# Key and receptance projections of an RWKV-7 mixer on Trainium2: rounded and low input streamed as one 512-column matmul, the two halves summed afterwards

## Chip, cores and metric

One core of one Trainium2 chip runs the whole program in one launch. The metric is device time in microseconds (us), the median of several executions, lower is better. Before the change it is 1180.07 us (three runs, 1178.05 to 1180.53).

## What is computed

A two-layer model on 256 tokens of width 2048: an RWKV-7 mixer, then sparse attention, in fp32. Only the first mixer is touched, and of it only how its key (k) and receptance (r) projections are summed up and handed on. Cut to what matters:

```python
def rwkv7_mixer(u, v_first, mu, w_rkvz, w0, w1, w2, a0, a1, a2, vres, k_k, k_a, r_k, ln_g, ln_b, w_o):
    xx = token_shift(u) - u
    mixed = u[None] + xx[None] * mu[:, None, None, :]
    rkvz = jnp.einsum('nbtd,nde->nbte', mixed[:4], w_rkvz)
    r, k, v, z = rkvz[0], rkvz[1], rkvz[2], rkvz[3]
    ...
    kk = heads(k * k_k).astype(jnp.float32)
    kk = kk / jnp.maximum(jnp.sqrt(jnp.sum(kk * kk, axis=-1, keepdims=True)), 1e-12)
    k = k * (1.0 + (a - 1.0) * k_a)
    ...
    o = wkv7_scan(rh, heads(decay), kh, vh, -kk, kk * ah.astype(jnp.float32))
```

## The kernel before

**Three products for one.** TensorE works on operands rounded to fp32r. Each fp32 factor is therefore split into a rounded ("high") part, made by ScalarE (L204 for weights: tile `whi`; L418 for inputs), and the remainder ("low"), made by VectorE (L189: `wlo`; L419). A projection sums high times high, high times low and low times high; low times low is dropped. High and low part of one 128-channel slice of the input lie side by side in one tile `mx` of 2 x 256 columns, named `joint[nm, k]` as a whole.

**Two ways to multiply.** `rows_step` (L568, L569, L571; v, z and the later products) loads the input as stationary operand and streams 512 weight columns. `cols_step` loads a 128x128 piece of the weight and streams the 256 tokens, so that the result lies with channels on partitions. Into a 256-column result it issues three matmuls of 256 columns for each of 16 slices (L587 `whi` times high, L588 `whi` times low, L589 `wlo` times high). Into a 512-column result it issues `whi` times the joint tile (512 columns, L593, or L596 for the last slice) and `wlo` times high into the first 256 columns (L594); the two halves are then still to be added. Before the change only the gate projection of the attention layer, late in the program, takes the second way.

**Key stage.** `phase_k(j)` makes block j of 16 (128 channels) in 16 slices. Two blocks share one 512-column bank of PSUM. Between the blocks stand the four blocks `phase_z` of the gate z; the last, `phase_z3`, follows k block 15. Each finished k block feeds `stage_k(j)`, a chain over all engines: ScalarE copies k to SBUF (L683, `ksb`) and squares it (L684, `t`), TensorE sums the squares (L687), VectorE and GpSimd take the power (L695, L696 `rnt`), ScalarE widens it (L702 `rnx`), TensorE turns it (L705), VectorE makes `nk` and `an` (L717 to L719), GpSimd scales (L724, L725 into `sp`), TensorE multiplies (L732), ScalarE copies out (L735 `abs`), and SyncE stores `sp` and `abs` to DRAM (L727 `spd`, L736 `abd`).

**Handover.** Within `phase_z3`, when all 16 chains are issued, the tiles of the scan are opened in the memory of the key stage, and what the scan needs first is loaded: `spl` from `spd` (L883), `invA` from `abd` (L763), `Yb` from `yvd` (L861), all on SyncE's queue, `a` and `t` on GpSimd's (L851, L853). The scan's first matmul (L976) reads `Yb`.

**Scan stage.** Eight pairs U of blocks go through twelve slots each (`phase`, `stats`, `finish`, `prep`, `scale_r`). Between the pieces of a slot `fill(n)` runs n slices of the r projection, block j into bank `rps[j % 2]`, and later of the output projection. `scale_r(U, x)` (slots 1 and 6) takes a finished r block from PSUM and multiplies it twice on VectorE (L964 into `spl`, L965 into `mb`); then GpSimd copies `pc` and makes `ars` (L966, L967).

**What sets the order.** In the key stage the framework orders every engine's instructions by its own timeline estimate. In the scan the order is that of the code, on all engines. In both each engine then runs its list in order, and SyncE's and GpSimd's DMA issues are items of such lists.

Of the kernel before, what the change touches and what calls it, by code (L numbers as in the profile page):

```python
# [10 lines left out]
F32 = mybir.dt.float32  # L11
F32R = mybir.dt.float32r
AF = mybir.ActivationFunctionType
OP = mybir.AluOpType
# [3 lines left out]
T, D, NK = 256, 2048, 16  # L18
# [197 lines left out]
def hybrid_kernel(ctx: ExitStack, tc: tile.TileContext, a: dict, out: bass.AP):  # L216
    nc = tc.nc
    V, S, G, PE = nc.vector, nc.scalar, nc.gpsimd, nc.tensor
# [35 lines left out]
    def accp(name="acc"):  # L254
        n = turn.get(name, 0)
        turn[name] = n + 1
        b = role[name]
        return psum.tile([128, 512], F32, name=f"bank{b[n % len(b)]}", bufs=1)
# [104 lines left out]
    def C(name):  # L363
        o, n = COLS[name]
        return cst[:, o:o + n]
# [17 lines left out]
    KK = prm0[:, 112:128]  # L383
# [197 lines left out]
    def cols_step(o, nm, q, first=True, **kw):  # L581
        wh, wl = W.get()
        for s in range(4):
            k = 4 * q + s
            mh, ml = need((nm, k))
            if o.shape[1] == T:
                PE.matmul(o, wh[:, s, :], mh, start=k == 0 and first, stop=False, **kw)  # L587
                PE.matmul(o, wh[:, s, :], ml, start=False, stop=False, **kw)  # L588
                PE.matmul(o, wl[:, s, :], mh, start=False, stop=k == NK - 1, **kw)  # L589
            else:  # L590
                end = k == NK - 1
                if not end:
                    PE.matmul(o, wh[:, s, :], joint[nm, k], start=k == 0, stop=False, **kw)  # L593
                PE.matmul(o[:, :T], wl[:, s, :], mh, start=False, stop=False, **kw)  # L594
                if end:
                    PE.matmul(o, wh[:, s, :], joint[nm, k], start=False, stop=True, **kw)  # L596
            yield 3 * N256

    def cols_block(nm, o):
        for q in range(4):  # L600
            yield from cols_step(o, nm, q)
# [46 lines left out]
    kph = tc.alloc_tile_pool(name="kph", bufs=1)  # L648
# [5 lines left out]
    kps, w2 = {}, {}  # L654
    kdone, a1done, tdone = set(), set(), set()

    def load_pair(u):
        t = kph.tile([LORA, 2, 256], F32, name="w2s", bufs=2)
        nc.sync.dma_start(t[:, 0, :], a["a_w2"][0][:, u * 256:(u + 1) * 256])
        nc.sync.dma_start(t[:, 1, :], a["a_a2"][0][:, u * 256:(u + 1) * 256])  # L660
        w2[u] = t
# [3 lines left out]
    def stage_k(j):  # L665
        PE, V, S, G = Ranked(nc.tensor, "skPE"), Ranked(nc.vector, "skE"), Ranked(nc.scalar, "skE"), Ranked(nc.gpsimd, "skE")
        yield lambda: j in kdone and (j < KLAG or (j - KLAG) in a1done)
        tmp = lambda name, bufs=2: kph.tile([128, T], F32, name=name, bufs=bufs)
        sp = kph.tile([128, SPW], F32, name="sp", bufs=3)
        BK = sp[:, 0:512].rearrange("p (c x t) -> p c x t", c=NCH, x=2)  # L670
        pp = sp[:, 512:512 + NCH * (CH + 1)].rearrange("p (c t) -> p c t", c=NCH)
        kr = sp[:, SPW - 512:SPW - 256]
        at = sp[:, SPW - 256:]
        w2t = w2[j // 2]
        sc = (j % 2) * 128
        la = accp("la")
        PE.matmul(la[:, :256], w2t[:, 0, sc:sc + 128], hw, start=True, stop=True)
        PE.matmul(la[:, 256:], w2t[:, 1, sc:sc + 128], ha, start=True, stop=True)
        sch.t += 860
        pk = kps.pop(j)  # L680
        ksb = tmp("ksb")
        sqk = tmp("t1")
        S.activation(ksb, pk, AF.Copy)  # L683
        S.activation(sqk, pk, AF.Square, scale=KK[:, j:j + 1])  # L684
        rn = accp("rn")
        for tt in range(2):
            PE.matmul(rn[:, 256 + 2 * tt:258 + 2 * tt], sqk[:, tt * 128:(tt + 1) * 128], C("bo"), start=True, stop=True)  # L687
        sch.t += 430
        yield 400.0
        sst = kph.tile([128, 2, 2], F32, name="sst", bufs=2)  # L690
        rnt = kph.tile([128, 2, 2], F32, name="rnt", bufs=2)
        thw, tha = tmp("thw"), tmp("tha")
        S.activation(thw, la[:, :256], AF.Tanh, scale=0.5, bias=W0H[:, j:j + 1])
        S.activation(tha, la[:, 256:], AF.Tanh, scale=0.5, bias=A0H[:, j:j + 1])
        V.tensor_scalar(sst, rn[:, 256:260].rearrange("p (a b) -> p a b", a=2), 1e-24, None, op0=OP.max)  # L695
        G.tensor_tensor(rnt, sst, half[:, 0:4].rearrange("p (a b) -> p a b", a=2), op=OP.pow)  # L696
        S.activation(thw, thw, AF.Copy, scale=0.5, bias=0.5)
        cum = tmp("cum")
        V.tensor_tensor_scan(cum, C("rst"), thw, 0.0, op0=OP.mult, op1=OP.add)
        yield 1000.0  # L700
        rnx = tmp("rnx")
        S.activation(rnx.rearrange("p (a b n) -> p a b n", a=2, b=2),  # L702
                     rnt[:, :, :, None].to_broadcast([128, 2, 2, 64]), AF.Copy)
        for tt in range(2):
            PE.transpose(rn[:, tt * 128:(tt + 1) * 128], rnx[:, tt * 128:(tt + 1) * 128], ident)  # L705
        sch.t += 215
        G.memset(pp[:, :, 0:1], 1.0)
        S.activation(pp[:, :, 1:], c3(cum), AF.Exp, scale=-DECAY)
        pinv = tmp("pinv")
        S.activation(pinv, cum, AF.Exp, scale=DECAY)  # L710
        an, f = tmp("an"), tmp("f")
        S.activation(an, tha, AF.Copy, scale=-0.5, bias=-0.5)
        S.activation(f, tha, AF.Identity, scale=KAH[:, j:j + 1], bias=KAM[:, j:j + 1])
        V.tensor_tensor(f, ksb, f, op=OP.mult)
        yield 800.0
        nk = tmp("nk")
        V.scalar_tensor_tensor(nk, ksb, KKN[:, j:j + 1], rn[:, :256], op0=OP.mult, op1=OP.mult)  # L717
        V.tensor_tensor(c3(at), c3(nk), pp[:, :, 0:CH], op=OP.mult)
        V.tensor_tensor(an, nk, an, op=OP.mult)  # L719
        S.activation(kr, f, AF.Copy, scale=RK[:, j:j + 1])  # L720
        yield 600.0
        for h in range(2):
            r = slice(64 * h, 64 * h + 64)
            G.tensor_tensor(BK[r, :, h, :], c3(an)[r], c3(pinv)[r], op=OP.mult)  # L724
            G.tensor_tensor(BK[r, :, 1 - h, :], c3(f)[r], c3(pinv)[r], op=OP.mult)  # L725
        yield 2500.0
        nc.sync.dma_start(spd[j], sp)  # L727
        ab = accp("ab")
        for c in range(NCH):
            for h in range(2):  # L730
                r = slice(64 * h, 64 * h + 64)
                PE.matmul(ab[r, c * 64:c * 64 + 64], c3(at)[r, c, :], BK[r, c, h, :], start=True, stop=True)  # L732
        sch.t += 700
        abs_ = tmp("abs")
        S.activation(abs_, ab[:, :256], AF.Copy)  # L735
        nc.sync.dma_start(abd[j], abs_)  # L736
        a1done.add(j)

    kacc = []

    def phase_k(j):
        if j % 2 == 0:
            load_pair(j // 2)
            kacc[:] = [accp("acc")]
        o = kacc[0][:, (j % 2) * 256:(j % 2) * 256 + 256]
        yield from cols_block("k", o)
        kps[j] = o
        kdone.add(j)

    def stage_t(b):  # L750
# [143 lines left out]
    for j in range(16):  # L894
        sch.add(stage_k(j))
# [8 lines left out]
    scan = tc.alloc_tile_pool(name="scan", bufs=1, reuse_waits="tile")  # L904
# [3 lines left out]
    rps = [accp() for _ in range(2)]  # L908
# [8 lines left out]
    mb = one("mb", [128, 2, T])  # L917
# [34 lines left out]
    def parts(U, x):  # L952
        t = SPL[U % 2][x]
        return (t[:, 0:512].rearrange("p (c x t) -> p c x t", c=NCH, x=2),
                t[:, 512:512 + NCH * (CH + 1)].rearrange("p (c t) -> p c t", c=NCH),
                t[:, SPW - 512:SPW - 256],
                t[:, SPW - 256:].rearrange("p (x c t) -> p x c t", x=2, c=NCH))

    def scale_r(U, x):
        if x == 0:  # L960
            PCH[U] = scan.tile([128, 2, NCH], F32, name="pc", bufs=3)
        BK, pp, kr, ar = parts(U, x)
        pr = rps[x][:, 0:256]
        V.tensor_tensor(ar[:, 1], c3(pr), pp[:, :, 1:], op=OP.mult)  # L964
        V.tensor_tensor(mb[:, x], pr, kr, op=OP.mult)  # L965
        G.tensor_copy(PCH[U][:, x], pp[:, :, CH])  # L966
        G.tensor_tensor(ARS[U % 2][x], ar[:, :, 1:, :],  # L967
                        pp[:, None, 0:NCH - 1, CH:CH + 1].to_broadcast([128, 2, NCH - 1, CH]), op=OP.mult)
# [169 lines left out]

    def stream():
        for j in range(NK):  # L1140
            yield from cols_block("r", rps[j % 2][:, 0:256])
        phase_done.add("r")
        banks(acc=(0, 1))
        for nb, k0, k1 in OSEQ:
            yield from o_part(nb, k0, k1)
# [284 lines left out]
    pr = accp("PT")  # L1430
# [284 lines left out]
```

## Time and profile before

| | |
|---|---|
| median of three runs | 1180.07 us (1178.05 to 1180.53) |
| the profiled execution's own time | 1183.66 us |
| its span (first to last instruction) | 1181.6 us |
| mean granted TensorE clock | 0.98 of full |
| busy: TensorE / VectorE / ScalarE / GpSimd | 1133.4 / 861.1 / 711.4 / 344.5 us |
| key stage with z blocks 0 to 2 | 145 to 325 us of the span |
| z block 3 (`phase_z3`) | 325 to 350 us |
| handover, TensorE idle | 350 to 360 us |
| scan with the r projection | 360 to 560 us |

Names in the rows: PE is TensorE, PEld its weight loads, DVE VectorE, ACT ScalarE, POOL GpSimd, SPq SyncE's queue. A row of the timeline has start, duration, engine, line, operation, output<-inputs, shape, and in brackets the idle time before it and what ended it. Matmuls are pipelined: the distance between two starts, not the duration, is what one costs.

### The profile page before, as it was taken

The page shows a single profiled execution, that of the slowest core. Times are in us where ns is not written, and L with a number is a line of the kernel's source. Part 1 is how long each engine was busy: PE and PEld are TensorE (multiplying, and loading weights), DVE is VectorE, ACT ScalarE, POOL GpSimd, SP SyncE. Part 2 cuts the span into 40 slices and gives each one's busy share as a digit, 9 for nine tenths or more (in the row PEclk, how much of TensorE's full clock was granted, in tenths as well). Part 3 has the DMA queues.
Part 4 walks back from the last instruction along what each step waited for, and adds up shares of the span by engine and source line. Part 5 has one row for each costly group of instructions (what it writes and reads, how often), then busy time and mean ns, then how long its engine had stood idle before and what let it go on. Part 6 is the DMA issues. An engine that isn't in the chain of part 4 may idle for free.

```text
span 1181.6 us, 25078 instructions
## 1 busy us (share of the span) xinstructions
PE 1133.4 (96%) x9160; PEld 975.2 (83%) x9160; DVE 861.1 (73%) x1915; ACT 711.4 (60%) x1680; POOL 344.5 (29%) x429
## 2 busy tenths in 40 slices
PE   8999999999986999999989999999999999999997
PEld 7788899887966988888668888787889888988887
DVE  6999877589795786666555868574476888887564
ACT  5667877667763345555445867574556666665553
POOL 1400046234554255654000001100234334344111
PEclk9999999999997999999899999999999999999999
DMA  6558887886888668684346768585655453744753
GB/s 223 172 180 244 239 224 224 227 215 189 261 240 203 182 165 244 181 221 141 99 144 211 248 185 270 167 293 166 183 152 142 126 134 97 191 110 143 287 194 107
DMA packets 232762, 225.22 MB, mean 191 GB/s; under 512 B 51344, under 2 KB 180672, under 8 KB 232256
## 3 DMA queue, kind: packets, MB, share of 16 engines
q1 hardware_dynamic: 228000, 219.01, 63.1%
q0 software_dynamic: 4640, 4.62, 1.7%
q8 instruction: 72, 1.18, 0.4%
q14 instruction: 50, 0.41, 0.1%
HBM read 200.48 MB, written 23.10 MB: 189 GB/s over the span
## 4 chain that ended last, share of the span: by engine, by line
PE 75%; DVE 11%; DMA 4%; issue 3%; ACT 3%; POOL 2%; SPq 1%; ACTq 0%; POOLq 0%; DVEq 0%
PE bank L569 12%; PE bank L568 12%; PE bank L571 12%; PE bank L232 5%; PE bank L593 5%; PE bank L587 4%; PE bank L589 3%; PE bank L588 3%; DVE wlo L189 3%; PE bank L594 3%; PE pair L571 1%; PE pair L568 1%; PE pair L569 1%; DMA invA<-abd 1%; ACT whi L204 1%
## 5 line engine op out<-in xcount | busy, mean ns | idle before, releaser
L189 DVE TENSOR_TENSOR wlo<-wraw,whi 128x512 fp32r<-128x512 f32 (+2 forms) x616 | 442.8, 732 | 145.9 <-ACT whi L204 142.2
L204 ACT ACTIVATE whi<-wraw 128x512 fp32r<-128x512 f32 (+2 forms) x664 | 401.8, 619 | 195.9 <-PE bank L571 96.4
L569 PE MATMUL bank<-wlo,mx 128*128 128x512 f32 (+3 forms) x608 | 230.1, 380 | 5.2 <-DVE wlo L189 5.2
L571 PE MATMUL bank<-whi,mx 128*128 128x512 f32 (+3 forms) x608 | 228.5, 378 | 0.0
L568 PE MATMUL bank<-whi,mx 128*128 128x512 f32 (+3 forms) x608 | 204.1, 379 | 1.2 <-ACT whi L204 1.1
L587 PE MATMUL bank<-mx,whi 128*128 128x256 f32 (+1 forms) x544 | 167.1, 307 | 0.3 <-ACT mx L418 0.3
L589 PE MATMUL bank<-mx,wlo 128*128 128x256 f32 (+1 forms) x544 | 156.2, 288 | 0.6 <-DVE wlo L189 0.6
L588 PE MATMUL bank<-mx,whi 128*128 128x256 f32 (+1 forms) x544 | 156.0, 287 | 0.0
L569 PEld LDWEIGHTS bank<-wlo,mx 128*128 128x128 f32 x608 | 114.8, 189 | 24.4 <-DVE wlo L189 6.7
L568 PEld LDWEIGHTS bank<-whi,mx 128*128 128x128 f32 x608 | 114.1, 189 | 19.9 <-ACT whi L204 1.5
L571 PEld LDWEIGHTS bank<-whi,mx 128*128 128x128 f32 x608 | 114.7, 189 | 17.5
L189 POOL TENSOR_TENSOR wlo<-wraw,whi 128x512 fp32r<-128x512 f32 (+2 forms) x48 | 62.4, 1301 | 168.2 <-ACT whi L204 135.5
L587 PEld LDWEIGHTS bank<-mx,whi 128*128 128x128 f32 (+1 forms) x544 | 104.2, 192 | 5.7 <-ACT mx L418 0.7
L589 PEld LDWEIGHTS bank<-mx,wlo 128*128 128x128 f32 (+1 forms) x544 | 104.4, 192 | 1.9 <-DVE wlo L189 1.0
L588 PEld LDWEIGHTS bank<-mx,whi 128*128 128x128 f32 (+1 forms) x544 | 104.8, 193 | 0.9
L593 PE MATMUL bank<-mx,whi 128*128 128x512 f32 x240 | 87.0, 398 | 0.0
L569 PE MATMUL bank<-wlo,kvh 128*128 128x512 f32 x192 | 76.9, 401 | 0.0
L571 PE MATMUL bank<-whi,kvl 128*128 128x512 f32 x192 | 76.1, 396 | 0.0
L594 PE MATMUL bank<-mx,wlo 128*128 128x256 f32 x256 | 70.7, 285 | 0.0
L568 PE MATMUL bank<-whi,kvh 128*128 128x512 f32 x192 | 67.4, 396 | 0.0
L418 ACT ACTIVATE mx<-mtmp 128x256 fp32r<-128x256 f32 x96 | 39.0, 413 | 28.0 <-DVE mtmp L425 27.3
L593 PEld LDWEIGHTS bank<-mx,whi 128*128 128x128 f32 x240 | 45.1, 188 | 8.8
(332 smaller groups left out, 2087.1 us busy)
## 6 DMA issues: line engine op xcount, KB each, us to landing
wraw<-in_a_w_rkvz_dram SPq DMA_DIRECT2D x128, 512.0 KB, 5.1
wraw<-in_kv_w_dram SPq DMA_DIRECT2D x48, 512.0 KB, 4.5
wraw<-in_b_w_in_dram SPq DMA_DIRECT2D x40, 512.0 KB, 4.1
wraw<-in_a_w_o_dram SPq DMA_DIRECT2D x32, 512.0 KB, 4.5
wraw<-in_b_w_o_dram SPq DMA_DIRECT2D x32, 512.0 KB, 3.6
spd<-sp SPq DMA_DIRECT2D x16, 642.0 KB, 4.7
spl<-spd SPq DMA_DIRECT2D x16, 642.0 KB, 5.9
wraw<-in_b_w_in_dram SPq DMA_DIRECT2D x24, 384.0 KB, 3.3
```

Of the source, the lines that this page charges most:

```text
L189: eng.tensor_tensor(lv, src, hv.bitcast(F32), op=OP.subtract)
L204: self.nc.scalar.activation(hv, src, AF.Copy)
L232: return fn(*args, **kw)
L418: S.activation(h, src, AF.Copy)
L568: PE.matmul(o, mh[:, ts], wh[:, 0, :], start=k == ends[0], stop=False)
L569: PE.matmul(o, mh[:, ts], wl[:, 0, :], start=False, stop=False)
L571: PE.matmul(o, ml[:, ts], wh[:, 0, :], start=False, stop=k == ends[1])
L587: PE.matmul(o, wh[:, s, :], mh, start=k == 0 and first, stop=False, **kw)
L588: PE.matmul(o, wh[:, s, :], ml, start=False, stop=False, **kw)
L589: PE.matmul(o, wl[:, s, :], mh, start=False, stop=k == NK - 1, **kw)
L593: PE.matmul(o, wh[:, s, :], joint[nm, k], start=k == 0, stop=False, **kw)
L594: PE.matmul(o[:, :T], wl[:, s, :], mh, start=False, stop=False, **kw)
```

## The change

k and r blocks now go into whole 512-column banks, so `cols_step` takes its second way for them: per slice one matmul of 512 and one of 256 columns in place of three of 256, and two weight loads in place of three. The halves are added afterwards: for k by a 512-column copy on ScalarE (`k2`) and an add on GpSimd, in `phase_k`, and the chain reads the sum from SBUF; for r by a 256-column copy on ScalarE (`rsum`) and an add on VectorE, in `scale_r`, where the product `mb` moves from VectorE to GpSimd. Line numbers behind the places of the edit shift by up to two.

```diff
@@ stage_k
-        pk = kps.pop(j)
-        ksb = tmp("ksb")
+        ksb = kps.pop(j)
         sqk = tmp("t1")
-        S.activation(ksb, pk, AF.Copy)
-        S.activation(sqk, pk, AF.Square, scale=KK[:, j:j + 1])
+        S.activation(sqk, ksb, AF.Square, scale=KK[:, j:j + 1])
@@ phase_k
         if j % 2 == 0:
             load_pair(j // 2)
-            kacc[:] = [accp("acc")]
-        o = kacc[0][:, (j % 2) * 256:(j % 2) * 256 + 256]
+        o = accp("acc")
         yield from cols_block("k", o)
-        kps[j] = o
+        ksb = kph.tile([128, T], F32, name="ksb", bufs=2)
+        k2 = kph.tile([128, 2 * T], F32, name="k2", bufs=1)
+        S.activation(k2, o, AF.Copy)
+        G.tensor_tensor(ksb, k2[:, :T], k2[:, T:], op=OP.add)
+        kps[j] = ksb
@@ scale_r
-        pr = rps[x][:, 0:256]
+        pr = scan.tile([128, T], F32, name="rsum", bufs=2)
+        S.activation(pr, rps[x][:, T:], AF.Copy)
+        V.tensor_tensor(pr, rps[x][:, :T], pr, op=OP.add)
         V.tensor_tensor(ar[:, 1], c3(pr), pp[:, :, 1:], op=OP.mult)
-        V.tensor_tensor(mb[:, x], pr, kr, op=OP.mult)
+        G.tensor_tensor(mb[:, x], pr, kr, op=OP.mult)
@@ stream
-            yield from cols_block("r", rps[j % 2][:, 0:256])
+            yield from cols_block("r", rps[j % 2])
```

The framework orders the key stage anew. On TensorE, late in `phase_z3`, the matmuls of the last chain (j = 15, L732, output `bank_4337`) stood here before, among z's matmuls (outputs `bank_4211` and `bank_4212`):

```order
L568 MATMUL bank_4211<-whi,mx_1329 128x512
L568 MATMUL bank_4212<-whi,mx_1329 128x512
L732 MATMUL bank_4337<-sp 64x64
L569 MATMUL bank_4211<-wlo,mx_1329 128x512
L571 MATMUL bank_4211<-whi,mx_1329 128x512
L569 MATMUL bank_4212<-wlo,mx_1329 128x512
L732 MATMUL bank_4337<-sp 64x64 x7
```

and in the changed kernel (there L730, `bank_4121`; z's outputs are `bank_3997` and `bank_3998`; L977 is the scan's first matmul):

```order
L730 MATMUL bank_4121<-sp 64x64 x7
L569 MATMUL bank_3997<-wlo,mx_1361 128x512
L571 MATMUL bank_3997<-whi,mx_1361 128x512
L569 MATMUL bank_3998<-wlo,mx_1361 128x512
L571 MATMUL bank_3998<-whi,mx_1361 128x512
L568 MATMUL bank_3997<-whi,mx_1376 128x512
L569 MATMUL bank_3997<-wlo,mx_1376 128x512
L571 MATMUL bank_3997<-whi,mx_1376 128x512
L568 MATMUL bank_3998<-whi,mx_1376 128x512
L569 MATMUL bank_3998<-wlo,mx_1376 128x512
L571 MATMUL bank_3998<-whi,mx_1376 128x512
L977 MATMUL pair_4429<-Yb_4225,a_4221 64x32 x16
```

Of the 96 matmuls of `phase_z3`, 77 stood ahead of the end of the last chain's matmuls (two of them even ahead of k block 15's end) and 19 behind it; now 86 stand ahead and 10 behind.

On GpSimd, the end of the key stage before (L696 is a chain's power, L725 and L724 its two scalings, L880 the first memset of the handover):

```order
L724 TENSOR_TENSOR sp<-an,pinv 64x4x64 x4
L725 TENSOR_TENSOR sp<-f,pinv 64x4x64 x2
L696 TENSOR_TENSOR rnt<-sst,half 128x4
L724 TENSOR_TENSOR sp<-an,pinv 64x4x64 x2
L880 MEMSET a_4437 128x512
```

and now (L694 is the power, L723 and L722 the scalings, L745 the new add; this one is that of block 15):

```order
L745 TENSOR_TENSOR ksb<-k_3994 128x256
L722 TENSOR_TENSOR sp<-an,pinv 64x4x64 x2
L723 TENSOR_TENSOR sp<-f,pinv 64x4x64 x2
L722 TENSOR_TENSOR sp<-an,pinv 64x4x64 x2
L694 TENSOR_TENSOR rnt<-sst,half 128x4
L722 TENSOR_TENSOR sp<-an,pinv 64x4x64 x2
L879 MEMSET a_4221 128x512
```

The add of a block stands in the same list as the scalings of the chains ahead of it (here of blocks 13, 14 and 15), and the chain of its own block starts behind it.

On SyncE's queue, around the store of the last chain's `abs`, before:

```order
L736 DMA abd<-abs 128x256 x2
L176 DMA wraw<-in_a_w_rkvz_dram 128x8x128 x3
L727 DMA spd<-sp 128x1284
L176 DMA wraw<-in_a_w_rkvz_dram 128x8x128 x2
L736 DMA abd<-abs 128x256
L883 DMA spl_4442<-spd 128x1284
L883 DMA spl_4443<-spd 128x1284
```

and now (L725 stores `sp`, L734 `abs`, L882 loads `spl`):

```order
L734 DMA abd<-abs 128x256
L176 DMA wraw<-in_a_w_rkvz_dram 128x8x128
L725 DMA spd<-sp 128x1284
L176 DMA wraw<-in_a_w_rkvz_dram 128x8x128 x2
L734 DMA abd<-abs 128x256
L882 DMA spl_4226<-spd 128x1284
L882 DMA spl_4227<-spd 128x1284
```

The neighbours of the last store are the same kinds; six loads of r weights (`wraw`) now stand ahead of it in all, where five did. In the scan the order is the old one but for the edited instructions, and ahead of the key stage and behind the scan nothing has moved.

More of the change, by code (lines that the diff above doesn't have):

```diff
@@ L737, in stage_k @@
         a1done.add(j)
-    kacc = []
     def phase_k(j):
```

## Prediction

> **What bounds the kernel now.** I read the page's busy times first, then the table of stretches around the two stages that change, then the handover between them row by row.
>
> ```profile
> span 1181.6 us, 25078 instructions
> PE 1133.4 (96%) x9160; PEld 975.2 (83%) x9160; DVE 861.1 (73%) x1915; ACT 711.4 (60%) x1680; POOL 344.5 (29%) x429
> ```
>
> TensorE is busy for 96% of the span. Where it is not idle, its work sets the time; whatever shortens that work counts only up to the next wait that something else ends.
>
> ```profile
> 145.00:325.00 180.00, 175.13 (x1318) 158.23 (x1317) 138.83 (x261) 125.71 (x286) 77.38 (x89) 1.00 0.78 223
> 325.00:350.00 25.00, 25.00 (x148) 19.65 (x146) 24.22 (x49) 17.23 (x40) 13.05 (x18) 1.00 0.81 236
> 350.00:361.00 11.00, 0.69 (x4) 0.28 (x2) 2.85 (x7) 2.20 (x5) 7.84 (x15) 0.66 0.88 232
> 361.00:385.00 24.00, 20.09 (x227) 19.12 (x228) 16.66 (x58) 8.92 (x18) 8.69 (x17) 0.86 0.85 200
> 385.00:560.00 175.00, 169.70 (x3269) 151.13 (x3267) 119.12 (x314) 90.59 (x264) 86.56 (x143) 0.97 0.70 190
> ```
>
> Columns: stretch, length, busy time of PE, PEld, DVE, ACT, POOL, granted TensorE clock, DMA share, GB/s. Key stage, z block 3, handover, the scan's start, the scan. The key stage and the scan are bound by TensorE (4.9 of 180 and 5.3 of 175 us idle). The third row is different: TensorE does next to nothing for 10 us. What ends that:
>
> ```profile
> 324.66 0.28 PE L589 MATMUL bank<-mx,wlo 128*128 128x256 f32 x1
> ...
> 345.92 0.37 ACT L735 ACTIVATE abs<-bank 128x256 f32<-128x256 f32 x1
> 346.65 0.53 SPq L736 DMA_DIRECT2D abd<-abs  x1
> 349.91 0.39 PE L571 MATMUL bank<-whi,mx 128*128 128x512 f32 x1
> 352.97 0.32 SPq L883 DMA_DIRECT2D spl<-spd  x1
> 353.82 5.96 DMA invA<-abd
> 360.28 0.39 PE L976 MATMUL pair<-Yb,a 64*64 64x32 f32 x2 [9.98 <-DMA Yb<-yvd]
> ```
>
> k block 15 ends at 324.66. Its chain ends with `abs` at 345.92; the store of it goes out at 346.65; the second load of `spl` (its memory lies over `abs`) goes out only at 352.97, when that store has landed; then `invA` and `Yb` behind it, and the scan starts at 360.28. z block 3 was done at 349.91, so the scan's start hangs on the last chain: 13.6 us behind its store, whatever TensorE has saved before.
>
> **The price of one slice.** Three 256-column matmuls as they stand in the key stage, and the new form as the attention layer already uses it:
>
> ```profile
> 203.01 0.28 PE L589 MATMUL bank<-mx,wlo 128*128 128x256 f32 x1
> 203.13 0.28 PE L587 MATMUL bank<-mx,whi 128*128 128x256 f32 x1
> 203.25 0.28 PE L588 MATMUL bank<-mx,whi 128*128 128x256 f32 x1
> 203.37 0.28 PE L589 MATMUL bank<-mx,wlo 128*128 128x256 f32 x1
> ...
> 989.91 0.39 PE L593 MATMUL bank<-mx,whi 128*128 128x512 f32 x1
> 990.14 0.28 PE L594 MATMUL bank<-mx,wlo 128*128 128x256 f32 x1
> 990.26 0.39 PE L593 MATMUL bank<-mx,whi 128*128 128x512 f32 x1
> ```
>
> Start to start: 0.36 us for three; 0.23 + 0.12 = 0.35 us for the pair. The columns are the same 768, so only about 10 ns per slice are to be had: 512 columns at 0.23 cost 10 ns less than twice 0.12. The weight load that drops out lay beside the matmuls and is worth nothing by itself. A saving of a third, as the count of instructions suggests, is not on offer. The number of slices, from the key stage (145 to 340 us) and from the scan (361 to 561 us):
>
> ```profile
> L587 PE MATMUL bank<-mx,whi 128*128 128x256 f32 x256 | 75.1, 293 | 0.0
> ...
> L587 PE MATMUL bank<-mx,whi 128*128 128x256 f32 x256 | 82.8, 323 | 0.0
> ```
>
> So at most 256 x 10 ns = 2.6 us in each stage.
>
> [...]
>
> **Key stage: what is added.**
>
> ```profile
> L683 ACT ACTIVATE ksb<-bank x16: 362/366/385, 151.4 to 325.9; 128x256 f32<-128x256 f32 x16
> L684 ACT ACTIVATE t<-bank,prm x16: 461/468/477, 151.6 to 326.2; 128x256 f32<-128x256 f32 x16
> L888 ACT ACTIVATE vt<-bank x1: 599/599/599, 349.7 to 349.7; 128x512 f32<-128x512 f32 x1
> L1471 POOL TENSOR_TENSOR zT<-zT,RST x16: 727/746/1196, 863.4 to 1084.0; 128x256 f32<-128x256 f32 x16
> L724 POOL TENSOR_TENSOR sp<-an,pinv x32: 728/1062/2922, 162.1 to 342.1; 64x256 f32<-64x256 f32 x32
> L719 DVE TENSOR_TENSOR an<-nk,an x16: 410/418/966, 160.5 to 339.8; 128x256 f32<-128x256 f32 x16
> ```
>
> (Durations are lowest/median/highest in ns.) Per block ScalarE swaps a 0.37 us copy for a 512-column one of 0.60: 16 x 0.23 = 3.7 us more, beside TensorE, on an engine with 54 us free of 180. GpSimd gets 16 adds of 0.75 us, 12 us, on an engine with 100 free. What lies on the chain: 0.60 + 0.75 in place of 0.37, so each chain gets about 1.0 us longer before the square (0.47, as before). The edges of the add are 0.73 and, queued behind a pair of scalings, 2 x 2.9 more. By the new order the squares' matmul stands some 28 to 31 matmuls of the next block behind its own block's end, about 14 slices or 5 us; 0.60 + 0.75 + 0.47 fits in with 3 us to spare, so TensorE should not wait there. Blocks in whole banks: no wait of TensorE in this stretch names a bank's release, so I take zero both ways. The waits it does have:
>
> ```profile
> PE bank L732 <- POOL sp L724: 1.7, 2, 1.3
> PE bank L687 <- ACT t L684: 1.3, 2, 1.1
> PE bank L705 <- ACT rnx L702: 1.2, 2, 0.8
> ```
>
> (Who waited for whom, total us, times, longest.) 4.2 us; the new order could remove all of them or, with a busier GpSimd, double them. I take no change, and keep -4.2 and +4.2 for the range.
>
> The handover then decides what of the 2.6 us arrives. Ahead of the last chain's last matmul TensorE does 256 cheaper slices (-2.6 us) but nine more matmuls of z block 3 (86 in place of 77, 9 x 0.23 = +2.1 us). So the store of `abs` goes out about 0.5 us sooner, and the scan starts 0.5 us sooner; z block 3 ends 2.6 us sooner, and the idle time grows from 10 to about 12 us. The sixth weight load ahead of that store waits for VectorE's low part of the first r piece, made beside z block 3 while the matmuls run; I take zero and, if it is late, up to the 3 us that VectorE (24.2 of 25 us busy there) could be behind. The memsets and loads of GpSimd at the handover hold `t`, which the scan needs only after its first step. **Key stage: -0.5 us.**
>
> **Scan: what is added.**
>
> ```profile
> 382.52 0.41 DVE L964 TENSOR_TENSOR spl<-bank,spl 128x256 f32<-128x256 f32 x1
> 383.32 0.27 PE L1011 MATMUL bank<-spl 64*64 64x64 f32 x2 [1.87 <-DVE mb L965]
> ...
> 420.70 0.70 ACT L1111 ACTIVATE O<-pair,nmr,rg 128x64 f32<-128x64 f32 x2 [1.83 <-DVE nmr L1097]
> 425.25 0.49 PE L1049 MATMUL pair<-X,Yb 64*64 64x64 f32 x8 [0.75 <-DVE sta L1079]
> ...
> 384.00:388.00 4.00, 4.00 (x63) 3.71 (x58) 3.73 (x14) 0.97 (x2) 1.02 (x3) 0.57 0.37 99
> 424.00:430.00 6.00, 5.25 (x82) 4.62 (x80) 4.00 (x11) 3.46 (x12) 0.00 (x0) 0.72 0.48 151
> ```
>
> VectorE does two passes of 0.41 us per block as before: the add comes in, `mb` goes out. ScalarE's copy (0.37 us, as L683) stands in slot 1 ahead of the `O` pieces, where ScalarE sat idle for 1.83 us until `nmr` was there, and in slot 6 behind `X`; 16 x 0.37 = 6 us on an engine with 84 free of 175. If that cover is gone, 8 x 0.37 = 3 us at the most. The bank is now free after copy and add, not after both products: at 383.32 TensorE waited for `mb`; it should wait about 0.4 us less. GpSimd's `mb` costs 16 x 0.75 = 12 us of its 88 free, and is read six slots later. Its one price: VectorE's 128x256 product took 0.42 us as a rule and 0.97 at worst, beside GpSimd; 16 such blows are 8.8 us of VectorE's time, of which only what falls into the few slots where TensorE waits for VectorE counts, as at 425.25. I take 0.4 us, with 0 and 2 as ends.
>
> Of the 2.6 us of the slices I take off what falls under half clock behind such waits (the last two rows, 0.57 and 0.72 granted) and into those slots, about a fifth: -2.1 us. With the 0.4: **scan -1.7 us.**
>
> Sum: -0.5 - 1.7 = -2.2 us, on a span of 1181.6 or an own time of 1183.66 us. That execution was 3.6 us over the median of the runs; taken from the median the forecast is 1180.07 - 2.2 = 1177.9 us. Measurement can tell about 0.2%, 2.4 us: below 1177.7 counts as faster, above 1182.4 as slower.
>
> **Rivals.**
>
> *The key stage's saving arrives too.* If half of the 4.2 us of waits go (the squares' matmul stands later than before), the last chain ends 2 us sooner still: 1175.8. For it: the new places are later. Against: the other two waits, on L705 and L732, are no nearer to gone.
>
> *GpSimd makes the last chain late (slower).* GpSimd runs its list in order. The add of a block stands among scalings that take up to 2.9 us each and that wait for VectorE's `an`:
>
> ```profile
> POOL sp L724 <- DVE an L719: 24.2, 10, 7.9
> ```
>
> An add behind such a wait holds the block's own chain; five or more blocks late by a microsecond push the store of `abs` back by 5 us, and the scan with it: 1177.9 + 0.5 + 5 = 1183.4. It decides from a store about 4 us later than in the forecast, near 350 us. Against: the order leaves 3 us of room at each block.
>
> [...]
>
> [...]
>
> **How the numbers follow.** The forecast 0.48, its own range 1176.3 to 1179.5 (the key stage's waits by 1, the scan's terms by 0.6); the saving arriving too 0.20; GpSimd late 0.22; nothing saved 0.10. Faster: 0.20 of the first, 0.19 of the second: 0.39. Slower: 0.20 of the third and 0.02 of the last: 0.22. The rest, 0.39, is within 0.2%. The range leaves a tenth on each side: 1175.0 to 1183.4.
>
> **What would show it.** In the profile after: pairs 0.35 us apart; z block 3 done near 347 us, the store of `abs` near 346 and the scan's first matmul near 359.8, with 12 us of idle ahead of it; waits of L685 on `t` gone; the r projection done some 2 us sooner relative to the scan's start. The prediction is wrong if TensorE waits for GpSimd's `ksb` in the key stage, if the store of `abs` leaves after 349, or if VectorE's waits in slot 3 grow past a microsecond more in sum.

## The result, and the profile after

The changed kernel took 1194.78 us (median of four runs, 1193.8 to 1200.13), the kernel before 1180.3 us beside it: ratio 1.0127, 95% interval 1.0102 to 1.0152. The forecast was 1177.9, its range ended at 1183.4. The change costs 14.5 us. Two single runs of the experiments below, 1213.6 us with `mb` back on VectorE and 5806 us in the last combined kernel, lie far off the others of their kernels and are left out of the figures.

The profiled execution took 1200.13 us, 5 to 6 us more than the other three; 2 us of that lie ahead of the key stage, where the two kernels do the same. Its span and busy times:

```profile
span 1198.4 us, 24104 instructions
PE 1134.9 (95%) x8648; PEld 944.4 (79%) x8648; DVE 865.6 (72%) x1915; ACT 717.1 (60%) x1696; POOL 379.2 (32%) x461
```

512 matmuls fewer, and TensorE is as busy as before. A second execution of it (1194.06 us, span 1192.3) is nearer to the median; its table of stretches, in the columns of the table of before (length, busy time of PE, PEld, DVE, ACT, POOL, granted clock, DMA share, GB/s):

```profile
145.00:321.20 176.20, 172.49 (x1050) 143.60 (x1049) 137.71 (x255) 123.83 (x276) 89.38 (x100) 0.99 0.78 222
321.20:349.80 28.60, 27.80 (x159) 21.51 (x158) 26.33 (x55) 19.34 (x47) 16.54 (x20) 1.00 0.75 226
349.80:362.60 12.80, 0.20 (x1) 0.00 (x0) 3.42 (x8) 2.84 (x6) 10.24 (x19) 0.60 0.94 256
362.60:386.40 23.80, 18.82 (x150) 15.32 (x150) 15.38 (x53) 9.19 (x20) 7.12 (x13) 0.86 0.79 161
386.40:570.00 183.60, 173.58 (x3090) 138.04 (x3090) 124.81 (x318) 94.44 (x276) 103.11 (x160) 0.95 0.70 183
```

Row by row against before: the key stage is 3.5 us shorter (179.7 to 176.2); z block 3 is 3.3 us longer (25.25 to 28.6), the idle time from its end to the scan's first matmul 2.7 us longer (10.37 to 13.03), and so the scan starts 2.4 us later, where it was to start 0.5 us sooner. Then the last row: TensorE idles 10.0 us in it instead of 5.3, and its granted clock is 0.95 instead of 0.97. So most of the loss is in the scan; from the end of the r projection to the end of the program the two take the same (622.2 and 622.5 us).

The key stage and the handover in the first profile, start and duration:

```profile
170.05 0.39 PE L593 MATMUL bank<-mx,whi 128*128 128x512 f32 x1
170.28 0.28 PE L594 MATMUL bank<-mx,wlo 128*128 128x256 f32 x1
170.40 0.39 PE L593 MATMUL bank<-mx,whi 128*128 128x512 f32 x1
...
324.75 0.40 PE L596 MATMUL bank<-mx,whi 128*128 128x512 f32 x1
...
352.43 0.37 ACT L733 ACTIVATE abs<-bank 128x256 f32<-128x256 f32 x1
353.17 1.34 SPq L734 DMA_DIRECT2D abd<-abs  x1
353.18 0.39 PE L571 MATMUL bank<-whi,mx 128*128 128x512 f32 x1
...
366.46 0.39 PE L977 MATMUL pair<-Yb,a 64*64 64x32 f32 x2 [12.89 <-DMA Yb<-yvd]
```

The pair costs 0.35 us, as forecast. The last `abs` comes 27.7 us behind the last slice of k (21.3 before), and the scan's first matmul 13.3 us behind the store (13.6 before).

Now one round of the scan where it goes wrong, in the first profile. GpSimd first, `mb` of slot 6 to `rg`; then VectorE, ScalarE and TensorE behind it (bracket: idle time and what ended it):

```profile
412.25 0.92 POOL L966 TENSOR_TENSOR mb<-rsum,spl 128x256 f32<-128x256 f32 x1 [8.50 <-issue]
...
414.70 0.59 POOL L850 DMA_DIRECT2D a<-abd  x1
...
418.51 0.55 POOL L852 DMA_DIRECT2D t<-tnd  x1
419.39 1.09 POOL L860 DMA_DIRECT2D Yb<-yvd  x2 [0.33 <-PE pair L1050]
421.93 0.55 POOL L860 DMA_DIRECT2D Yb<-yvd  x1 [1.45 <-DMA a<-abd]
423.76 2.82 POOL L860 DMA_DIRECT2D Yb<-yvd  x5 [1.28 <-DMA vt<-vd]
426.59 2.08 POOL L1091 TENSOR_TENSOR rg<-rg,half 128x8 f32<-128x8 f32 x1
```

```profile
424.13 0.17 DVE L1090 TENSOR_SCALAR rg<-mv 128x8 f32<-128x8 f32 x1
...
428.70 0.17 DVE L1098 SCALAR_TENSOR_TENSOR nmr<-mv,rg 128x8 f32<-128x8 f32 x1 [1.57 <-POOL rg L1091]
...
430.06 0.28 DVE L1064 COPY S<-pair 128x128 f32<-128x128 f32 x1
```

```profile
428.90 0.70 ACT L1112 ACTIVATE O<-pair,nmr,rg 128x64 f32<-128x64 f32 x2 [3.31 <-DVE nmr L1098]
...
430.39 0.56 PE L1043 MATMUL pair<-S,ars 64*64 64x64 f32 x16 [2.25 <-DVE S L1064]
```

In the kernel before, the same eight `Yb` loads went out in one piece and `rg` found GpSimd waiting for it:

```profile
413.02 4.33 POOL L861 DMA_DIRECT2D Yb<-yvd  x8 [2.17 <-PE pair L1049]
418.02 2.05 POOL L1090 TENSOR_TENSOR rg<-rg,half 128x8 f32<-128x8 f32 x1 [0.67 <-DVE rg L1089]
```

So `mb` stands ahead of eight DMA issues, these stand ahead of eight more, and `rg` stands behind them all. And in the trace the second eight wait for landings: the four loads of `a` took 2.8 to 7.0 us from issue to landing, and GpSimd stood idle 1.45 us ahead of the third load of `Yb` until one of them had landed, and 1.28 us ahead of the fourth, which the profile puts down to a landing of `vt`. From 385 to 560 us its waits ahead of loads of `Yb` that ended with a landing of `a` sum up to 4.2 us in the first profile and 6.0 in the second, and to 0.9 in the kernel before. Why the issue of one load waits for the landing of another was not shown.

This seemed to be the whole cause. The first four runs showed that it was not.

### The profile page after: what moved, and what is told of

Same layout as the page of the kernel before. It is cut to its first block, busy times and chain, and to the rows that moved or that the text cites. A ratio compares the mean times of both kernels' runs of the same rounds, so it can differ in the third digit from the quotient of the medians.

```text
span 1198.4 us, 24104 instructions
## 1 busy us (share of the span) xinstructions
PE 1134.9 (95%) x8648; PEld 944.4 (79%) x8648; DVE 865.6 (72%) x1915; ACT 717.1 (60%) x1696; POOL 379.2 (32%) x461
## 4 chain that ended last, share of the span: by engine, by line
PE 53%; DMA 4%; DVE 2%; issue 2%; ACT 2%; POOL 1%; SPq 0%; POOLq 0%; ACTq 0%; DVEq 0%
PE bank L569 9%; PE bank L571 9%; PE bank L568 9%; PE bank L593 7%; PE bank L232 5%; PE bank L594 3%; DMA a<-abd 2%; DMA Yb<-yvd 1%; PE pair L571 1%; PE pair L568 1%; PE pair L569 1%; DVE wlo L189 1%; POOL Yb L860 1%; ACT whi L204 1%; PE pair L1056 1%
## 5 line engine op out<-in xcount | busy, mean ns | idle before, releaser
L593 PE MATMUL bank<-mx,whi 128*128 128x512 f32 x720 | 276.9, 418 | 0.0
L594 PE MATMUL bank<-mx,wlo 128*128 128x256 f32 x768 | 214.0, 288 | 3.8 <-DVE wlo L189 3.8
L568 PE MATMUL bank<-whi,mx 128*128 128x512 f32 (+3 forms) x608 | 204.7, 379 | 1.4 <-ACT mx L418 0.9
L593 PEld LDWEIGHTS bank<-mx,whi 128*128 128x128 f32 x720 | 137.8, 192 | 29.3
L594 PEld LDWEIGHTS bank<-mx,wlo 128*128 128x128 f32 x768 | 147.9, 193 | 9.4 <-DVE wlo L189 5.0
L425 DVE SCALAR_TENSOR_TENSOR mtmp<-xx,prm,xn 128x256 f32<-128x256 f32 x96 | 48.6, 519 | 1.1 <-POOL xx L457 1.0
L569 PEld LDWEIGHTS bank<-wlo,kvh 128*128 128x128 f32 x192 | 36.1, 188 | 8.5 <-issue 0.4
L419 DVE TENSOR_TENSOR mx<-mtmp,mx 128x256 fp32r<-128x256 f32 x96 | 41.5, 442 | 1.4 <-ACT mx L418 1.4
L1045 ACT ACTIVATE X<-pair 128x128 f32<-128x128 f32 x32 | 8.9, 279 | 56.0 <-PE pair L1043 33.9
L571 PEld LDWEIGHTS bank<-whi,kvl 128*128 128x128 f32 x192 | 36.2, 188 | 7.4
```

The lines of the kernel that those rows point to most:

```text
L419: V.tensor_tensor(l, src, h.bitcast(F32), op=OP.subtract)
L425: V.scalar_tensor_tensor(m, xx[:, k, :], mu[:, k:k + 1], xn[:, k, 1:], op0=OP.mult, op1=OP.add)
L568: PE.matmul(o, mh[:, ts], wh[:, 0, :], start=k == ends[0], stop=False)
L569: PE.matmul(o, mh[:, ts], wl[:, 0, :], start=False, stop=False)
L571: PE.matmul(o, ml[:, ts], wh[:, 0, :], start=False, stop=k == ends[1])
```

## The experiments

Each was timed beside the kernel before (its medians there 1180.2 to 1181.4); the ratio is to that. "r stretch" is first to last matmul of the r projection: 195.0 us in the first profile of before, 206.0 and 203.0 in the two of the changed kernel.

### The parts alone

**Key part alone**: the edits in `scale_r` and `stream` undone.

> The key projection as changed, the receptance projection as before. Theory 1: the scan keeps its old pace (r projection 195 us from the scan's first matmul), and only the later scan start of about 4 us is left: 1184 us. If the later last abs does not matter, as a rival has it (the scan's start was late in that one execution alone): 1180 us.

1182.1 us, ratio 1.0006 (0.9987 to 1.0025): no change that the runs can tell, and between the two expectations. In its profile k takes 175.8 us, the last `abs` comes at 348.5, the scan starts at 362.55, the r stretch is 192.5. So the key stage does save 3.8 us, and the handover takes more than that back: counted from the start of k, the last `abs` comes 2.2 us later than before and the scan starts 1.8 us later.

**Receptance part alone**: the edits in `stage_k` and `phase_k` undone.

> The receptance projection as changed, the key projection as before. Theory 1: the scan starts where it did (360 us), the r projection takes 206 us: 1190.5 us (1189 to 1192). If the scan's slower pace comes from its later start or from what the key stage left behind, it is gone here: 1180 us or less.

1188.5 us, 1.0056 (1.0035 to 1.0077). The scan starts at 360.3 and the r stretch is 199.6: slower, if by less than expected. The cost is 7 us, the key part's 0.7, and the two together cost 14.5: they do not add up. The scan from 23.8 us behind its start, in the columns of the table above and with as many matmuls as its last row (this execution took 1185.8 us):

```profile
384.10:564.60 180.50, 168.58 (x3090) 134.31 (x3090) 125.10 (x319) 94.23 (x276) 103.05 (x160) 0.98 0.71 186
```

TensorE idles 11.9 us of it.

### The scan: two causes, each hiding the other

**`mb` back on VectorE.**

```diff
-        G.tensor_tensor(mb[:, x], pr, kr, op=OP.mult)
+        V.tensor_tensor(mb[:, x], pr, kr, op=OP.mult)
```

> The changed kernel with one line undone: the product mb is back on VectorE; the r halves are still summed behind TensorE, the key stage is as changed. Theory 1 (GpSimd's list): mb's 0.9 us on GpSimd holds the scan's loads of a and Yb and then the power of rg behind them; without it the r projection takes about 195 us from the scan's first matmul instead of 206, and the time is near 1184 us (1182 to 1186). Theory 2 (the longer link): the ScalarE copy and the VectorE add of the halves hold the scan; then this edit, which puts a third pass on VectorE, gains nothing: 1193 us or more. [...]

1193.6 us, 1.0105 (1.006 to 1.015). Theory 1 alone falls, the time is the one that theory 2 expected: the r stretch is 200.8, TensorE's waits for `Yb` within the scan are down to 1.1 us (5.2 and 3.1 in the two profiles of the changed kernel), but it waits 4.8 us for `S` and 7.4 us for `sta`.

**GpSimd's part of slot 6 behind the loads** (in part; `scale_g` holds the three GpSimd operations, the comment is added here).

```diff
             if v == 6 and U + 2 < NU:
                 load_a(U + 2)
+            if v == 6 and U + 1 < NU:
+                scale_g(U + 1, 1)    # mb, pc, ars of the second half
```

> The changed kernel, with the same work on every engine, but in slot 6 GpSimd's three operations of the second half (mb, pc, ars) stand behind the eight DMA issues of a and t instead of ahead of them. Theory 1: the loads go out as early as before, Yb and rg follow in time, and the scan's loss of about 11 us goes but for 1 to 3: 1186 us (1184 to 1188). [...]

1197.8 us, 1.0134 (1.0094 to 1.0175), r stretch 204.7. No gain either. What still holds the scan is seen in slot 1; the kernel before first, then the kernel with `mb` on VectorE:

```profile
523.24 0.42 DVE L964 TENSOR_TENSOR spl<-bank,spl 128x256 f32<-128x256 f32 x1
...
524.16 0.57 ACT L1051 ACTIVATE uv<-pair 64x128 f32<-64x128 f32 x2 [0.73 <-PE pair L1049]
526.14 0.17 DVE L1097 SCALAR_TENSOR_TENSOR nmr<-mv,rg 128x8 f32<-128x8 f32 x1 [1.55 <-POOL rg L1090]
...
526.82 0.28 DVE L1063 COPY S<-pair 128x128 f32<-128x128 f32 x1
```

```profile
505.72 0.57 ACT L1052 ACTIVATE uv<-pair 64x128 f32<-64x128 f32 x2 [0.72 <-PE pair L1050]
506.32 0.39 ACT L963 ACTIVATE rsum<-bank 128x256 f32<-128x256 f32 x1
506.73 0.42 DVE L964 TENSOR_TENSOR rsum<-bank,rsum 128x256 f32<-128x256 f32 x1 [1.81 <-ACT rsum L963]
...
508.47 0.16 DVE L1098 SCALAR_TENSOR_TENSOR nmr<-mv,rg 128x8 f32<-128x8 f32 x1
...
509.15 0.28 DVE L1064 COPY S<-pair 128x128 f32<-128x128 f32 x1
```

Before, VectorE's products started 0.9 us ahead of `uv`. Now ScalarE's copy of the second half stands behind `uv`, which waits for TensorE; VectorE idles 1.81 us for it, and `S` follows `uv` by 3.43 us instead of 2.66 (in this kernel VectorE's third pass stands in between as well). The last matmul of the r block had started at 502.63, 3.7 us ahead of the copy: nothing but the place in ScalarE's list makes the copy wait.

**The copy for slot 1 one slot earlier; and that with `mb` on VectorE** (in part; `scale_r` then takes this copy and makes none of its own in slot 1, the comment is added here).

```diff
                 if U + 1 < NU:
+                    copy_r(U + 1, 0)     # S.activation(rsum, rps[0][:, T:], AF.Copy)
                     load_v(U + 1)
```

> The changed kernel, with the ScalarE copy of the r half for slot 1 made one slot earlier, behind X and ahead of uv, since the r block is complete by then; mb stays on GpSimd. Theory 4 (the copy's place in ScalarE's list): in the changed kernel the copy stands behind uv, which waits for TensorE, so VectorE idles some 1.8 us ahead of its add in each round and nmr, S and O come late; with the early copy these waits of VectorE for rsum go (8.4 us in sum), and what is left is GpSimd's mb ahead of the loads and of rg: the r projection takes 198 to 202 us instead of 206, the time is 1187 to 1191 us. Theory 1 (GpSimd alone): no change, 1194 us or more.

1195.7 us, 1.0109 (1.0077 to 1.0141), r stretch 203.4. VectorE's waits for `rsum` in the rounds are gone, but now `nmr` waits for `rg` (7.8 us in sum from 385 to 560 us, 0.5 in the second profile of the changed kernel). The gain is smaller than theory 4 expected; `mb` still stands ahead of the loads.

The second kernel has this and the edit of `mb` above.

> The changed kernel with both: the copy for slot 1 made one slot earlier, and mb back on VectorE. Theory 4 with 1 (two causes, each of which keeps the scan late when the other is taken away): the r projection takes 192 to 195 us, and only the key stage's part is left: 1180 to 1182 us. If a third pass of VectorE per block is what counts (theory 5): 1188 us or more, with VectorE busy without idle time between rg and S.

1185.05 us, 1.0052 (1.0026 to 1.0079), r stretch 192.8. No cure by itself gained more than some 5 us of the stretch, and none gained time that the runs can tell; the two together gain 10 us of the stretch at the least and 10 us of time.

**Both moved, the work on every engine unchanged**: the early copy, and GpSimd's part of slot 6 behind the loads.

> The changed kernel with two moves and the same work on every engine: the ScalarE copy for slot 1 one slot earlier, and GpSimd's mb, pc and ars of slot 6 behind the DMA issues of a and t. mb stays on GpSimd. If GpSimd's part of the loss is only that mb stands ahead of these loads: the r projection takes 193 to 197 us, the time is 1185 to 1188 us, as with mb back on VectorE (192.8, 1185). [...]

1180.8 us, 0.9985 (0.9967 to 1.0003), r stretch 191.0. `mb` is on GpSimd, all operations are those of the change, and 14 us are gone by two moves, one of a copy and one of GpSimd's three operations. So `mb`'s own time on GpSimd does not count wherever it stands; its place was the mistake. The time is 4 us better than with `mb` on VectorE, but there `pc` and `ars` stayed ahead of the loads, and how much of the 4 us is theirs was not tested. The stretches of this kernel from the scan's start, the second one with the same 3090 matmuls as the last row of the changed kernel's table:

```profile
361.50:385.25 23.75, 19.19 (x164) 15.64 (x168) 15.64 (x54) 9.28 (x20) 7.09 (x13) 0.85 0.68 161
385.25:556.60 171.35, 166.51 (x3090) 132.89 (x3082) 128.65 (x318) 93.87 (x276) 100.07 (x160) 0.99 0.72 196
```

Against 183.6 us in the changed kernel: TensorE idles 4.8 us instead of 10.0, and the granted clock is 0.99 instead of 0.95, so that the same matmuls take 166.5 us of busy time instead of 173.6 (166.5 x 0.99 / 0.95 = 173.5). Of the 12.3 us, 5.2 are idle time and 7.1 are clock. And who waits for whom from 385 to 560 us, in the changed kernel (second profile) and in this one (total us, times, longest):

```profile
ACT O L1112 <- DVE nmr L1098: 8.8, 5, 2.2
DVE rsum L964 <- ACT rsum L963: 8.4, 5, 1.8
POOL Yb L860 <- DMA a<-abd: 6.0, 4, 2.5
PE pair L1050 <- DVE sta L1080: 5.2, 4, 2.2
```

```profile
POOL Yb L860 <- PE pair L1065: 23.3, 6, 5.0
ACT O L1127 <- DVE nmr L1113: 4.5, 6, 1.9
PE pair L1065 <- DVE sta L1095: 2.7, 4, 1.4
```

The loads of `Yb` now wait for TensorE to release their tile, and no longer for a landing. So it was in the kernel before:

```profile
POOL Yb L861 <- PE pair L1049: 11.2, 6, 2.2
```

**Receptance alone, with `mb` on VectorE and the early copy** (k as before, and the two edits shown).

> The key projection as before; the receptance projection as changed, with the early copy and mb on VectorE. If the two halves of the change add up: the scan starts at 360 us as in the kernel before, the r projection takes 192.5 us, and the time is 1178 us (1177 to 1179.5). If the scan's saving comes only together with the changed key stage, or the copy of the second half costs as much as it brings: 1180 us or more.

1185.0 us, 1.0027 (1.0014 to 1.004), r stretch 197.9: with `mb` on VectorE the receptance part does not pay even without the key part. Whether VectorE's third pass does it, or `pc` and `ars` ahead of the loads, no run separates.

**Receptance alone, with both moves** (k as before).

> The key projection as before; the receptance projection as changed, with the early ScalarE copy and GpSimd's mb, pc, ars of slot 6 behind the loads. The scan starts where it did, at 360 us; the r projection takes 191 to 193.5 us; the slices' 2 us arrive: 1178.5 us (1177 to 1180) against 1180.5 for the kernel before. If the saving of the scan comes only with the changed key stage ahead of it: 1181 us or more.

1178.4 us, 0.9978 (0.9965 to 0.9991), r stretch 190.3: the receptance part by itself, with its operations in these places, pays about 2.6 us.

### The key stage and its handover

In the three kernels of this section the receptance projection is as before.

**Halves added on VectorE.**

```diff
-        S.activation(k2, o, AF.Copy)
-        G.tensor_tensor(ksb, k2[:, :T], k2[:, T:], op=OP.add)
+        S.activation(ksb, o[:, T:], AF.Copy)
+        V.tensor_tensor(ksb, o[:, :T], ksb, op=OP.add)
```

> Only the key projection is changed, and its halves are added on VectorE (ScalarE copies 256 columns, VectorE adds them to the bank) instead of a 512-column copy on ScalarE and an add on GpSimd. In the order that the framework makes of it, 26 matmuls of z block 3 stand behind the last chain's, where 10 did with the GpSimd add and 19 in the kernel before. Theory A (the gain of the key stage is eaten at the handover by the last chain's place): the key stage keeps its 3.8 us, the last abs comes some 5 us earlier than in the kernel before, and the scan starts 3 to 5 us earlier: 1176 to 1178 us. Theory B (VectorE, not GpSimd, is short in z block 3): no gain, 1181 us or more.

1180.1 us, 1.000 (0.9984 to 1.0017). The last `abs` comes sooner than with GpSimd's add (346.5 against 348.5), though not sooner than before (345.9): the key stage is 2.7 us longer than with GpSimd's add (178.5), and TensorE waits in it once 3.9 us for `wlo` (2.6 with GpSimd's add). And the scan starts at 362.8 all the same, 15.8 us behind the store instead of 13.3. Neither theory: one part of the gain is paid for ahead of the handover, the other within it.

**Last block as before.**

```diff
-        yield from cols_block("k", o)
+        last = j == NK - 1
+        yield from cols_block("k", o[:, :T] if last else o)
...
+        if last:
+            S.activation(ksb, o[:, :T], AF.Copy)
```

> Only the key projection is changed, but its last block (j = 15) is summed on TensorE as before, with three matmuls a slice, and has neither the 512-column copy nor the GpSimd add on its chain. Its order puts only 5 matmuls of z block 3 behind the last chain's (10 with all blocks changed, 19 before). If the last chain's own copy and add make the handover late: the last abs comes 1 us or more earlier than with all blocks changed, 1180 us or less. If the order of TensorE's list does it: the last abs comes about 1 us later still, 1183 us.

1187.3 us, 1.0056 (1.0036 to 1.0075). The last `abs` comes 2.7 us later than with all blocks changed, counted from the start of k, though its chain has neither the 512-column copy nor the add: it is not these that make the handover late. The five further matmuls of z ahead of the last chain's end account for 1.2 us, and `abs` itself comes 1.1 us later behind its matmuls on ScalarE. The time is 4 us worse than that order explains; its profile, of an execution of 1184.7 us, does not show where.

**Last four blocks on VectorE.**

```diff
+        if j >= 12:
+            S.activation(ksb, o[:, T:], AF.Copy)
+            V.tensor_tensor(ksb, o[:, :T], ksb, op=OP.add)
+        else:
```

> Only the key projection is changed; the halves of blocks 0 to 11 are added on GpSimd as in the change, those of blocks 12 to 15 on VectorE (256-column copy and an add from the bank). In the order that results, 24 matmuls of z block 3 stand behind the last chain's, 10 with all adds on GpSimd, 19 before. Theory A (the place of the last chain in TensorE's list sets the scan's start): the key stage keeps its 3.5 us, the last abs comes about 3 us sooner than with all adds on GpSimd, the scan starts near 359.5 us instead of 362.6: 1178 to 1180 us. Theory B (the chain is late by GpSimd's and ScalarE's own work, not by that place): the scan starts at 362 us or later, 1182 us.

The last `abs` comes at 342.7, 4.3 us sooner counted from the start of k than with all adds on GpSimd, as theory A says, but the store and the loads behind it take longer:

```profile
343.35 1.03 SPq L734 DMA_DIRECT2D abd<-abs  x1
345.95 0.37 SPq L176 DMA_DIRECT2D wraw<-in_a_w_rkvz_dram  x1
346.41 4.21 SPq L886 DMA_DIRECT2D spl<-spd  x2
...
359.00 0.72 PE L979 MATMUL pair<-Yb,a 64*64 64x32 f32 x4 [11.74 <-DMA Yb<-yvd]
```

From store to scan it is 15.7 us instead of 13.3; the scan starts 2.1 us sooner. The time does not show even that: 1182.8 us, 1.0005 (0.9988 to 1.0022), where the profiled execution took 1178.5. So the key part is worth nothing in three of its four forms and costs some 7 us in the fourth, and what keeps the scan's earlier start out of the time stays open. A sooner store is at least not handed on in full: here and with all halves added on VectorE the scan starts 15.7 and 15.8 us behind it. The record does not show why.

### Together, and the baselines

Both parts; every key add on VectorE, the early copy, `mb` on VectorE:

> Both projections changed; the key halves added on VectorE, the receptance with the early copy and mb on VectorE. Key part alone measured 1180.1 against 1180.2 before; if the receptance part brings its 2 us on top: 1178 us. If the two parts disturb each other as in the changed kernel: 1183 us or more.

1186.1 us, 1.0031 (1.001 to 1.0053), r stretch 196.7: with `mb` on VectorE again no gain.

Both parts; the last four key adds on VectorE, the early copy, GpSimd's part of slot 6 behind the loads:

> Both projections as changed, with all mends: key adds of the last four blocks on VectorE; in the scan the early ScalarE copy, and GpSimd's three operations of slot 6 behind the loads. With all mends but the first it took 1180.8 us. If the mends add up: 1177 us (1176 to 1179). If the last chain's place brings nothing: 1180.5 us.

1179.6 us, 0.9982 (0.9969 to 0.9995): 2 us faster than before, but no better than the receptance part alone.

The changed kernel, and the kernel before, once more:

> The changed kernel once more, for a second profile of it (the first one fell on the longest of its four runs). Both theories: about 1194.5 us; the r projection takes 202 to 206 us from its first matmul, VectorE waits some 8 us for the rsum copy, and the scan starts 13 to 14 us behind the last abs.

1194.9 us, r stretch 203.0, VectorE's waits for `rsum` 8.4 us, the scan 13.8 us behind the last `abs`: as expected. It is the profile quoted as the second one above.

> The kernel before once more, for a second profile of it, since the first one took 3.6 us more than the median. Expected 1180 us; the scan's first matmul at 360 us as in the first profile; the r projection 190.5 to 193 us from its first matmul, less than the 195 of the first profile, if the forecast's own size for the scan's saving (1.7 us) is right; 195 us if the saving is 4.

One run, 1182.5 us; the scan's first matmul at 362.2, 215.5 us behind the start of k (215.3 in the first profile), r stretch 191.3. The first profile's 195.0 was long; the unchanged scan code gave 190.6 to 195.2 in six profiles (before twice, and the four kernels with the key part alone). A difference of under 5 us in one stretch of one profile is therefore no evidence here, and the conclusions above rest on the times.

## Why the prediction was wrong

- **The slice, and its sum: right, a little small.** Pairs 0.35 us apart; over the key stage the median distances in the traces are three times 120 ns before and 234 and 117 ns now, 9 ns less per slice, and in the scan a slice takes 7 ns less in the mean (415 in the kernel before, 408 with both moves, at full clock). The 0.10 on "nothing saved" supposed a slice that gains next to nothing; no run shows that, the traces show the 9 and 7 ns. The key stage is 3.5 us shorter in the second profile and 3.8 with the key part alone, but 2.0 in the first profile, instead of 2.6; of the 3.5, 1.2 are waits of TensorE that went (4.9 us idle before, 3.7 now; the rival "the saving arrives too" had this half right).
- **The handover: wrong in sign.** The step was "nine more matmuls of z block 3 (...) = +2.1 us". From the last slice of k to the last `abs` it is 6.6 us more in the second profile (27.8 against 21.3): 11 more matmuls of z from that point with their spacing, 3.2 us; eight more matmuls of other kinds and the spacing of the chains' own, 1.4; waits, 0.8, for VectorE's `wlo`; `abs` itself 1.2 later behind its matmuls on ScalarE. I counted one kind of matmul and took the rest of the list, and the waits in it, as equal. The store left at 349.6 and 353.2 in the two profiles, past the 349 that I had named as a sign, and the scan started 2.4 us later. Nor do the 13.6 us from store to scan hold "whatever TensorE has saved before": they were 15.7 and 15.8 in two kernels above.
- **`mb` on GpSimd: the step that failed.** "GpSimd's `mb` costs 16 x 0.75 = 12 us of its 88 free, and is read six slots later. Its one price: VectorE's 128x256 product" was wrong. The price named was small: in the first profile one of the sixteen products took 0.98 us, the others 0.42 to 0.44. The real one is what stands behind `mb` in GpSimd's list, 16 DMA issues and the power that `nmr`, `O` and `S` wait for; with the early copy in place, moving `mb`, `pc` and `ars` behind the first eight issues let the r stretch fall from 203.4 to 191.0 us. The free time was an average; the slack at that place was 0.67 us for `rg`, in a row that I could have read.
- **The ScalarE copy: the other step that failed.** "in slot 1 ahead of the `O` pieces, where ScalarE sat idle for 1.83 us" was true, and the bound of 3 us was not: I priced the copy's time on its own engine and did not ask what stands ahead of it (`uv`, waiting for TensorE) and who waits behind it (VectorE, 8.4 us). With GpSimd's part behind the loads, making the copy earlier brought the r stretch from 204.7 to 191.0 us.
- **The rival on the slow side** named GpSimd's list, in the wrong stage: key stage, 5 us. There ScalarE did wait for `ksb`, 8.9 us in the second profile, but TensorE waited only 0.3 us for the squares behind it (1.3 before).
- **What stays open.** Key part 0.7 and receptance part 7.1 us alone, 13.5 to 14.5 together: some 6 us of interplay. With both places mended there is none (1180.8), so it goes through these places. But TensorE's waits in the scan are not longer with both parts than with the receptance part alone: 10.0 us (second profile) against 11.9. What differs is that the scan starts 2.9 us later, counted from the start of k, and that the same matmuls take 5.0 us more at a clock of 0.95 instead of 0.98. Why the clock is lower was not settled.

## What to carry to other kernels

A moved or added operation costs what its queue makes of it: list what stands ahead of it and what it waits for, what stands behind it and who waits for that, DMA issues included; a share of free time answers neither. Two such waits in one loop can hide each other, so undo them together before a cause is dropped. And when the work is right but late, try another place before another engine.

## What the runs showed of the hardware

In the scan some short waits of TensorE were followed by a stretch at half clock. So it was behind the 2.25 us wait at 430.39 in the first profile of the changed kernel (columns as above):

```profile
424.00:430.40 6.40, 4.15 (x51) 3.11 (x49) 4.73 (x14) 2.79 (x9) 6.16 (x9) 1.00 1.08 248
430.40:434.00 3.60, 2.59 (x51) 2.33 (x52) 2.41 (x8) 3.60 (x12) 1.71 (x3) 0.53 0.89 294
434.00:438.00 4.00, 4.00 (x28) 3.01 (x29) 2.50 (x5) 1.61 (x5) 0.00 (x0) 0.57 0.12 27
```

In the second of these rows TensorE still waits for 1.0 us, in the third it does not wait at all and runs at 0.57. But not every wait was followed by one. The longest of the same scan, 2.36 us, was followed by 22 us at full clock:

```profile
462.59 0.34 PE L1050 MATMUL pair<-X,Yb 64*64 64x64 f32 x8 [2.36 <-DVE sta L1080]
462.60:484.90 22.30, 22.29 (x410) 17.70 (x410) 14.26 (x36) 9.79 (x30) 12.48 (x20) 1.00 0.96 251
```

Followed window by window, the granted clock of these scans is 1.00 or 0.50 (0.50 from 430.6 to 437.4 us in this one). Behind the first 24 us of the scan the stretches at 0.50 last 6.8, 6.8 and 3.4 us in the first profile of the changed kernel, and 3.4 us each, three of them, in the first profile of the kernel before. In sum they make up 17 us in each profile of the changed kernel and 3.4 in the kernel with both moves. Half of the difference, (17.0 - 3.4) / 2 = 6.8 us, is an estimate of its cost, beside the 7.1 us of busy time found above; 5.2 us were idle time. The forecast had allowed for the clock with a fifth of a small term. What starts such a stretch stays open: with the receptance part alone TensorE idled 11.9 us there and had 7 us at half clock.
